# Four scheduling edits in a two-layer attention trunk: halved weight casts, two earlier bias tables, earlier rotary tables, and the cosine product of the rotary step on GpSimd

## The chip, the cores and the metric

The kernel runs on one core of a Trainium2 chip as one launch. The metric is the device time of one execution in microseconds (us), the median over runs. TensorE (PE in the profile, its weight loads PEld) does the matrix products, VectorE is DVE, ScalarE is ACT, GpSimd is POOL, and SyncE (SP) issues most of the transfers; ACT issues the weight loads.

## What is computed

An encoder trunk of two layers over 1024 tokens of width 1024, all in float32. Layer A is chunked attention with 16 heads of 64 and a learned bias by relative distance; layer B is differential attention (two softmax maps for each of 8 heads, one subtracted from the other) with rotary positions on the first quarter of each head dimension. Cut to what matters here:

```python
def partial_rope(t, positions):
    ang = positions.astype(jnp.float32)[..., None] * inv_freq
    cos, sin = jnp.cos(ang), jnp.sin(ang)
    t1, t2 = t[..., :half], t[..., half:ROT_DIM]
    return jnp.concatenate([t1 * cos - t2 * sin, t2 * cos + t1 * sin, t[..., ROT_DIM:]], axis=-1)

# layer A
q, k, v, g = jnp.split(rmsnorm(h, a_norm_pre) @ a_w_in, 4, axis=-1)
bias = jnp.take(rel_bias, rel, axis=1)
s = jnp.einsum('bhqd,bhkd->bhqk', qc, kb) * scale + bias
h = h + rmsnorm((attention(s, v) * jax.nn.silu(g)) @ a_w_out, a_norm_post)
# layer B
ks_ = partial_rope(ks_, positions); q = partial_rope(q, positions)
a = p[:, :, 0] - lam * p[:, :, 1]
h = h + rmsnorm((rmsnorm(a @ v) * jax.nn.silu(g)) @ b_w_out, b_norm_post)
```

## The kernel before, in words

Every float32 product is made of three products of rounded parts: a weight or activation is cast to a high part on ACT (`hi_of`, L189) and the remainder is subtracted on DVE (`lo_of`, L192). A projection group (`mm_group`, L269, L271, L273) is 24 matmuls of 128x512 into one of two PSUM accumulators `acc`. Activations are kept transposed in R1 and R2.

The order of the work is written out by hand in **ticks** (class `Ticks`). One tick issues the work that is due before it (`at`), then 4 matmuls of the stream of projections (`FILL`), then the work due after it by rank (`after`, `later`). So a group lasts 6 ticks. `K.later(k, f, rank)` puts f k ticks on; each engine runs its instructions strictly in the order that results. The stream is projections A, output product A, projections B, output product B; the attention of a head pair is spread over the projections of the next.

What the change touches:
- `w_split` (L199 to L203): cast and remainder of one 128x1024 slice of layer A's weights, on tick 0 and 1. The first two slices are split before the projections start.
- `Prepared.prepare` (L230 to L249): the 32 slices of layer B's weights are scaled on POOL, cut into high and low part and stored to DRAM (`wcut`) during layer A.
- `bias_build` (L441 to L454): a head's bias table. A transfer brings the skewed table to the tile `b`, `part2` completes it on DVE (L448 to L450) 7 ticks later and SP stores it to `bias_t`. The scores of the head (`scores`, L606) read it back as `bt` (L635).
- `rope` (L884 to L903), called by `doneB` for the key (kind 0) and the query (kind 1) of a head pair, in two halves of 512 tokens. ACT copies `acc` to `xs`, four transfers on SP move the rotated rows to a tile `sw` (called `w` in the code), DVE writes `acc` times the cosine to `xc`, POOL multiplies `sw` by the sine at tick 3, DVE adds the two at tick 6 (5 for the first pair, u = 0), and one tick later the sum is split into parts (`split_k`, `split_q`). For the query, `split_q` also issues two transfers on SP that copy its parts to the other half of the partitions (L520, shown as R<-R).
- `layer_b_tiles` (L869 to L880): memsets and loads of the rotary tables and the mask, 6 ticks before layer B.
- `attB` (L917): when the attention blocks of layer B start; for u = 0 block i starts max(0, 1 - i) ticks late.

A scores product goes to the one PSUM tile `sp` (L597), so the next must wait until `scores` has read it. Transposes (L165) go to three PSUM tiles `tp`.

Of the kernel before, what the change touches and what calls it, by code (L numbers as in the profile page):

```python
# [11 lines left out]
F32 = mybir.dt.float32  # L12
# [94 lines left out]
def trunk(ctx, tc, x, positions, a_norm_pre, a_w_in, a_rel_rev, a_w_out, a_norm_post,  # L107
# [90 lines left out]

    def w_split(w):  # L199
        hi, lo = w_tile("whi"), w_tile("wlo")  # L200
        K.later(0, lambda: hi_of(w, hi), 2)
        K.later(1, lambda: lo_of(w, hi, lo), 2)
        return hi, lo  # L203

    class Weights:
# [18 lines left out]
    class Prepared:  # L224
# [5 lines left out]
        def prepare(self, k):  # L230
            view, n, gain = self.specs[k]
            w = mp.tile([P, D], F32, tag="h", name="w", bufs=4)
            w3 = w.rearrange("p (c n) -> p c n", n=P)
            adma(out=w3, in_=view[n])

            def cut():
                hi = mp.tile([P, D], F32, tag="h", name="wh", bufs=4)
                K.later(0, lambda: hi_of(w, hi.bitcast(F32R)))
                K.later(1, lambda: lo_of(w, hi.bitcast(F32R), w.bitcast(F32R)), 2)
                K.later(3, lambda: [dma(out=wcut[k][:, 0, :], in_=hi), dma(out=wcut[k][:, 1, :], in_=w)])  # L240

            def scaled(half):
                c = slice(half * 4, half * 4 + 4)
                G.tensor_tensor(out=w3[:, c, :], in0=w3[:, c, :],  # L244
                                in1=gain[:, c].unsqueeze(2).broadcast_to([P, 4, P]), op=ALU.mult)

            for half in range(2):
                K.later(6 + half, lambda half=half: scaled(half), 2)
            K.later(8, cut)  # L249
# [191 lines left out]
    def bias_build(h, k):  # L441
        def part1():
            b = mp.tile([P, D], F32, tag="h", name="b", bufs=4)
            dma(out=b[:, 384:640], in_=skew[h][127:127 + P * 382].rearrange("(p x) -> p x", x=382)[:, 0:256])
            K.later(7, lambda: part2(b))

        def part2(b):
            V.tensor_copy(out=b[:, 0:384], in_=b[:, 384:385].broadcast_to([P, 384]))  # L448
            V.memset(b[64:128, 0:64], NEG)
            V.memset(b[0:64, 576:640], NEG)  # L450
            dma(out=bias_t[h][NT], in_=b[:, 0:640])

        K.later(k, lambda: bias_skew(h))
        K.later(k + 4, part1)  # L454
# [426 lines left out]

    swc = [0]

    def rope(acc, half, first, then):  # L884

        cs = slice(half * 512, (half + 1) * 512)
        xs = lp.tile([P, 512], F32, tag="px", name="xs", bufs=3)
        xc = lp.tile([P, 512], F32, tag="px", name="xc", bufs=3)
        w = rot[swc[0] % 2]
        swc[0] += 1  # L890

# [4 lines left out]
                dma(out=w[m + 8:m + 16, :], in_=xs[m:m + 8, :])  # L896

        K.later(0, a)
        K.later(0, lambda: V.tensor_tensor(out=xc, in0=acc, in1=rot["cos"][:, cs], op=ALU.mult), 2)  # L899
        k = 5 if first else 6  # L900
        K.later(3, lambda: G.tensor_tensor(out=w, in0=w, in1=rot["sin"][:, cs], op=ALU.mult))  # L901
        K.later(k, lambda: V.tensor_tensor(out=xc, in0=xc, in1=w, op=ALU.add))
        then(xc, k + 1)  # L903

    def doneB(u, kind, half, acc):
        par = u % 2
        if kind == 0:
            rope(acc, half, u == 0, lambda xs, k: split_k(xs, ksB(par)[:, :, half * 512:half * 512 + 512], k))
        elif kind == 2:
            v = vvB(par, half).rearrange("p b (l n) -> p b l n", l=2)  # L910
            v_tokens(acc, lambda pt: pt.rearrange("p (b n) -> p b n", b=4), v[:, :, 0, :], v[:, :, 1, :])
        elif kind == 1:
            rope(acc, half, u == 0, lambda xs, k: split_q(xs, qqB, half, k))
        else:
            gate(acc, gB[u])

    def attB(u, base):  # L917
        par = u % 2
        for i in range(NT):
            attB_block(u, par, i, base + 6 * i + (max(0, 1 - i) if u == 0 else 0))  # L920

    def attB_block(u, par, i, t0):
        w = (i + 1) * P
# [153 lines left out]
    for k in range(32):  # L1077
        K.after(START + 30 + 21 * k // 2, lambda k=k: WB.prepare(k))
    K.after(start_b - 14, lambda: WB.load(0))
    K.after(start_b - 6, layer_b_tiles)  # L1080
    K.after(start_b - 11, lambda: WB.split(0))
    for O, w, R, t0, lead in ((OA, w_out_a, R1, out_a, 6), (OB, w_out_b, R2, out_b, 7)):
        wout(w, R, 0, t0 - 19)
# [99 lines left out]
```

## Time and profile before

| | |
|---|---|
| median of 3 runs | 1328.13 us (1327.79 to 1331.78) |
| the profiled execution | 1329.67 us |
| its span in the trace | 1327.8 us |
| PE busy | 1290.0 us, 97% |
| DVE, ACT, POOL busy | 826.2, 685.1, 450.2 us |

The span runs from the first to the last instruction that the trace shows; 1.9 us of the execution lie outside it. Layer A's projections and attention run to about 560 us of the span, its output product to 677, layer B's projections and attention to about 1190, and its output product to the end. In a view of waits, an instruction is followed by what it waited for; in a timeline a row gives start, duration, engine, line, operation and tiles, and in brackets the idle time of the engine just before it with what ended it. The granted clock of PE has two levels, 1.2 and 2.4 GHz, shown as 0.5 and 1.0.

### The profile page before, as it was taken

The page shows a single profiled execution, that of the slowest core. Times are in us where ns is not written, and L with a number is a line of the kernel's source. Part 1 is how long each engine was busy: PE and PEld are TensorE (multiplying, and loading weights), DVE is VectorE, ACT ScalarE, POOL GpSimd, SP SyncE. Part 2 cuts the span into 40 slices and gives each one's busy share as a digit, 9 for nine tenths or more (in the row PEclk, how much of TensorE's full clock was granted, in tenths as well). Part 3 has the DMA queues.
Part 4 walks back from the last instruction along what each step waited for, and adds up shares of the span by engine and source line. Part 5 has one row for each costly group of instructions (what it writes and reads, how often), then busy time and mean ns, then how long its engine had stood idle before and what let it go on. Part 6 is the DMA issues. An engine that isn't in the chain of part 4 may idle for free.

```text
span 1327.8 us, 20645 instructions
## 1 busy us (share of the span) xinstructions
PE 1290.0 (97%) x6919; PEld 1090.8 (82%) x6919; DVE 826.2 (62%) x1719; ACT 685.1 (52%) x1488; POOL 450.2 (34%) x688
## 2 busy tenths in 40 slices
PE   6899999999999999999997999999999999999997
PEld 5788888888888888888886888888888888888786
DVE  5466665656575656665434676757575758588643
ACT  5456575656565656654333454545454545456311
POOL 1146444555545454442221222212121212122321
PEclk8999999999999999999998999999999999999999
DMA  5477767776677778655443232323232323225343
GB/s 215 117 259 226 229 216 233 242 233 231 229 251 246 236 223 268 205 176 151 148 134 115 77 107 73 107 76 108 75 109 74 109 74 109 74 78 172 99 151 107
DMA packets 103094, 211.24 MB, mean 159 GB/s; under 512 B 14432, under 2 KB 49280, under 8 KB 102976
## 3 DMA queue, kind: packets, MB, share of 16 engines
q1 hardware_dynamic: 80448, 135.85, 32.7%
q10 hardware_dynamic: 22528, 73.95, 17.2%
q8 instruction: 57, 0.93, 0.3%
q14 instruction: 61, 0.50, 0.1%
HBM read 135.19 MB, written 58.83 MB: 146 GB/s over the span
## 4 chain that ended last, share of the span: by engine, by line
PE 80%; issue 5%; POOL 5%; DVE 3%; ACT 2%; DMA 2%; SPq 1%; ACTq 0%; POOLq 0%; DVEq 0%
PE acc L269 15%; PE acc L271 14%; PE acc L273 14%; PE acc L782 12%; PE sp L597 8%; PE tp L165 8%; PE av L981 4%; PE av L699 4%; POOL st L169 1%; POOL s L651 1%; DVE R L192 1%; POOL w L244 1%; DMA skew<-rev 1%; ACT R L189 1%; DMA sw<-xs 0%
## 5 line engine op out<-in xcount | busy, mean ns | idle before, releaser
L273 PE MATMUL acc<-R,wlo 128*128 128x512 f32 x1008 | 410.4, 407 | 0.0
L269 PE MATMUL acc<-R,whi 128*128 128x512 f32 x1008 | 405.4, 402 | 0.7 <-DVE xc L899 0.7
L271 PE MATMUL acc<-R,whi 128*128 128x512 f32 x1008 | 404.7, 401 | 0.1
L612 ACT ACTIVATE s<-s,st 128x640 f32<-128x640 f32 (+7 forms) x256 | 188.2, 735 | 135.1 <-DVE st L606 131.5
L192 DVE TENSOR_TENSOR R<-tp,R 128x512 fp32r<-128x512 f32 (+3 forms) x304 | 178.8, 602 | 85.3 <-ACT R L189 83.9
L169 POOL TENSOR_TENSOR st<-st,mone 128x1 f32<-128x1 f32 x192 | 128.2, 668 | 277.5 <-ACT s L612 254.9
L273 PEld LDWEIGHTS acc<-R,wlo 128*128 128x128 f32 x1008 | 191.1, 190 | 33.0
L271 PEld LDWEIGHTS acc<-R,whi 128*128 128x128 f32 x1008 | 191.4, 190 | 30.8 <-DVE R L192 0.4
L269 PEld LDWEIGHTS acc<-R,whi 128*128 128x128 f32 x1008 | 191.7, 190 | 29.0 <-DVE xc L899 1.1
L189 ACT CAST R<-tp 128x512 fp32r<-128x512 f32 (+3 forms) x304 | 155.3, 515 | 107.6 <-PE tp L165 104.3
L597 PE MATMUL sp<-R 128*128 128x256 f32 (+3 forms) x768 | 174.3, 335 | 10.5 <-DVE st L606 6.3
L606 DVE CUSTOM_DVE_ANT_0 s<-sp,mask 128x256 f32<-128x256 f32 (+7 forms) x128 | 96.6, 755 | 111.3 <-PE sp L597 111.2
L597 PEld LDWEIGHTS sp<-R 128*128 128x128 f32 x768 | 136.4, 189 | 32.4 <-DVE st L606 8.1
L782 PE MATMUL acc<-R,ohi 128*128 128x512 f32 x512 | 161.0, 394 | 0.0
L606 DVE CUSTOM_DVE_ANT_0 s<-sp,bt 128x640 f32<-128x640 f32 (+4 forms) x128 | 83.7, 654 | 75.0 <-PE sp L597 50.0
L165 PEld LDWEIGHTS tp<-ident,s 128*128 128x128 f32 x768 | 96.0, 140 | 39.1 <-DVE s L950 10.6
L165 PE MATMUL tp<-ident,s 128*128 128x128 f32 x768 | 124.1, 274 | 0.9 <-DVE s L950 0.8
L901 POOL TENSOR_TENSOR sw<-sw,sin 128x512 f32<-128x512 f32 x32 | 43.0, 1344 | 225.0 <-DMA sw<-xs 203.9
L782 PEld LDWEIGHTS acc<-R,ohi 128*128 128x128 f32 x512 | 94.7, 188 | 18.5
L178 POOL TENSOR_SCALAR st<-st 128x1 f32<-128x1 f32 x80 | 20.7, 259 | 242.7 <-ACT tt L185 190.0
L782 PE MATMUL acc<-R,olo 128*128 128x512 f32 x256 | 101.5, 397 | 0.0
L651 POOL TENSOR_SCALAR s<-s,st 128x640 f32<-128x640 f32 (+4 forms) x128 | 90.7, 708 | 12.6
(123 smaller groups left out, 1639.2 us busy)
## 6 DMA issues: line engine op xcount, KB each, us to landing
bt<-bias_t SPq DMA_DIRECT2D x64, 320.0 KB
R<-R SPq DMA_DIRECT2D x64, 256.0 KB
wcut<-wh SPq DMA_DIRECT2D x32, 512.0 KB
wcut<-w SPq DMA_DIRECT2D x32, 512.0 KB
whi<-wcut ACTq DMA_DIRECT2D x32, 512.0 KB
wlo<-wcut ACTq DMA_DIRECT2D x32, 512.0 KB
wst<-in_a_w_in_dram ACTq DMA_DIRECT2D x29, 512.0 KB
w<-in_kv_w_dram ACTq DMA_DIRECT2D x16, 512.0 KB
```

Of the source, the lines that this page charges most:

```text
L165: T.transpose(dst, src, ident)
L169: G.tensor_tensor(out=r, in0=a, in1=mone, op=ALU.pow)
L189: A.copy(out=hi, in_=src)
L192: V.tensor_tensor(out=lo, in0=src, in1=hi.bitcast(F32), op=ALU.subtract)
L269: T.matmul(acc, lhsT=hi[:, c, :], rhs=xT(0, c), start=(c == 0), stop=False)
L271: T.matmul(acc, lhsT=hi[:, c, :], rhs=xT(1, c), start=False, stop=False)
L273: T.matmul(acc, lhsT=lo[:, c, :], rhs=xT(0, c), start=False, stop=(c == NC - 1))
L597: T.matmul(sp[:, a:b], lhsT=q[:, l, (i % 4) * P:(i % 4 + 1) * P], rhs=ks[:, head, j0 * P + a - c0:j0 * P + b - c0], start=(l == 0), stop=( ...
L606: V.tensor_tensor_reduce(out=s[:, 0:w], in0=sp, in1=add, op0=ALU.add, op1=ALU.min, scale=-0.125, scalar=BIG, accum_out=mx)
L612: A.activation(s[:, 0:w], s[:, 0:w], AF.Exp, bias=mx, scale=-1.0, accum_out=sums)
L651: G.tensor_scalar(out=s[:, 0:w], in0=s[:, 0:w], scalar1=r, scalar2=0.5, op0=ALU.mult, op1=ALU.mult)
L782: T.matmul(y, lhsT=lhs[:, c, :], rhs=R[:, n * 8 + c, l * 512:(l + 1) * 512], start=(m == 0), stop=(m == 23))
```

## The change

The casts of a weight slice and of a prepared slice are made in two halves on successive ticks (and a prepared slice is stored one tick later). The first two bias tables are completed 4 ticks after their load and not 7. `layer_b_tiles` runs 40 ticks before layer B and not 6. In `rope` the cosine product moves from DVE (read from `acc`) to POOL (in place on `xs`, at tick 2), DVE's sum goes to `xs` too, always at tick 6, and the blocks of the first pair start one tick later.

```diff
@@ -198,8 +198,10 @@
 
     def w_split(w):
         hi, lo = w_tile("whi"), w_tile("wlo")
-        K.later(0, lambda: hi_of(w, hi), 2)
-        K.later(1, lambda: lo_of(w, hi, lo), 2)
+        for k in range(2):
+            c = slice(k * 4, k * 4 + 4)
+            K.later(k, lambda c=c: hi_of(w[:, c, :], hi[:, c, :]), 2)
+            K.later(k + 1, lambda c=c: lo_of(w[:, c, :], hi[:, c, :], lo[:, c, :]), 2)
         return hi, lo
 
     class Weights:
@@ -235,9 +237,11 @@
 
             def cut():
                 hi = mp.tile([P, D], F32, tag="h", name="wh", bufs=4)
-                K.later(0, lambda: hi_of(w, hi.bitcast(F32R)))
-                K.later(1, lambda: lo_of(w, hi.bitcast(F32R), w.bitcast(F32R)), 2)
-                K.later(3, lambda: [dma(out=wcut[k][:, 0, :], in_=hi), dma(out=wcut[k][:, 1, :], in_=w)])
+                for j in range(2):
+                    c = slice(j * 512, j * 512 + 512)
+                    K.later(j, lambda c=c: hi_of(w[:, c], hi[:, c].bitcast(F32R)), 2)
+                    K.later(j + 1, lambda c=c: lo_of(w[:, c], hi[:, c].bitcast(F32R), w[:, c].bitcast(F32R)), 2)
+                K.later(4, lambda: [dma(out=wcut[k][:, 0, :], in_=hi), dma(out=wcut[k][:, 1, :], in_=w)])
 
             def scaled(half):
                 c = slice(half * 4, half * 4 + 4)
@@ -442,7 +446,7 @@
         def part1():
             b = mp.tile([P, D], F32, tag="h", name="b", bufs=4)
             dma(out=b[:, 384:640], in_=skew[h][127:127 + P * 382].rearrange("(p x) -> p x", x=382)[:, 0:256])
-            K.later(7, lambda: part2(b))
+            K.later(4 if h < 2 else 7, lambda: part2(b))
 
         def part2(b):
             V.tensor_copy(out=b[:, 0:384], in_=b[:, 384:385].broadcast_to([P, 384]))
@@ -881,11 +885,10 @@
 
     swc = [0]
 
-    def rope(acc, half, first, then):
+    def rope(acc, half, then):
 
         cs = slice(half * 512, (half + 1) * 512)
         xs = lp.tile([P, 512], F32, tag="px", name="xs", bufs=3)
-        xc = lp.tile([P, 512], F32, tag="px", name="xc", bufs=3)
         w = rot[swc[0] % 2]
         swc[0] += 1
 
@@ -896,28 +899,27 @@
                 dma(out=w[m + 8:m + 16, :], in_=xs[m:m + 8, :])
 
         K.later(0, a)
-        K.later(0, lambda: V.tensor_tensor(out=xc, in0=acc, in1=rot["cos"][:, cs], op=ALU.mult), 2)
-        k = 5 if first else 6
+        K.later(2, lambda: G.tensor_tensor(out=xs, in0=xs, in1=rot["cos"][:, cs], op=ALU.mult))
         K.later(3, lambda: G.tensor_tensor(out=w, in0=w, in1=rot["sin"][:, cs], op=ALU.mult))
-        K.later(k, lambda: V.tensor_tensor(out=xc, in0=xc, in1=w, op=ALU.add))
-        then(xc, k + 1)
+        K.later(6, lambda: V.tensor_tensor(out=xs, in0=xs, in1=w, op=ALU.add))
+        then(xs, 6 + 1)
 
     def doneB(u, kind, half, acc):
         par = u % 2
         if kind == 0:
-            rope(acc, half, u == 0, lambda xs, k: split_k(xs, ksB(par)[:, :, half * 512:half * 512 + 512], k))
+            rope(acc, half, lambda xs, k: split_k(xs, ksB(par)[:, :, half * 512:half * 512 + 512], k))
         elif kind == 2:
             v = vvB(par, half).rearrange("p b (l n) -> p b l n", l=2)
             v_tokens(acc, lambda pt: pt.rearrange("p (b n) -> p b n", b=4), v[:, :, 0, :], v[:, :, 1, :])
         elif kind == 1:
-            rope(acc, half, u == 0, lambda xs, k: split_q(xs, qqB, half, k))
+            rope(acc, half, lambda xs, k: split_q(xs, qqB, half, k))
         else:
             gate(acc, gB[u])
 
     def attB(u, base):
         par = u % 2
         for i in range(NT):
-            attB_block(u, par, i, base + 6 * i + (max(0, 1 - i) if u == 0 else 0))
+            attB_block(u, par, i, base + 6 * i + (max(0, 2 - i) if u == 0 else 0))
 
     def attB_block(u, par, i, t0):
         w = (i + 1) * P
@@ -1077,7 +1079,7 @@
     for k in range(32):
         K.after(START + 30 + 21 * k // 2, lambda k=k: WB.prepare(k))
     K.after(start_b - 14, lambda: WB.load(0))
-    K.after(start_b - 6, layer_b_tiles)
+    K.after(start_b - 40, layer_b_tiles)
     K.after(start_b - 11, lambda: WB.split(0))
     for O, w, R, t0, lead in ((OA, w_out_a, R1, out_a, 6), (OB, w_out_b, R2, out_b, 7)):
         wout(w, R, 0, t0 - 19)
```

The order of the instructions moves with it. The transfers share eight semaphores in turn (DMAHW0 to DMAHW7); a transfer that takes one waits until its last user has landed. Line numbers of the changed kernel are its own. First SP's queue in the first 20 us of the projections, before, with the two rows of ACT's queue that load and cast a weight slice (`wst_1727`):

```order
L520 DMA R2_158<-R2_158 64x1024 [waits DVE_49,Activation_49]
L421 DMA lt_1701<-in_b_lambda_q1_dram 128x64 [waits DMAHW1_49]
L421 DMA lt_1701<-in_b_lambda_k1_dram 128x64
L423 DMA kvg_1395<-in_kv_norm_dram 128x8x1 [waits DMAHW6_49]
L424 DMA bng_1396<-in_b_norm_pre_dram 128x8x1 [waits DMAHW7_49]
L425 DMA fq_1397<-in_rope_freq_dram 128x1 [waits DMAHW0_49]
L635 DMA bt_1733<-bias_t0_75 128x128 [waits DMAHW1_49]
L215 DMA wst_1727<-in_a_w_in_dram 128x1024 [waits DVE_49]
L189 CAST whi_1771<-wst_1727 128x1024 [waits DMAHW1_49]
```

The same place now:

```order
L524 DMA R2_158<-R2_158 64x1024 [waits DMAHW7_49,DVE_49,Activation_49]
L425 DMA lt_1705<-in_b_lambda_q1_dram 128x64
L425 DMA lt_1705<-in_b_lambda_k1_dram 128x64
L427 DMA kvg_1395<-in_kv_norm_dram 128x8x1 [waits DMAHW5_49]
L428 DMA bng_1396<-in_b_norm_pre_dram 128x8x1 [waits DMAHW7_49]
L429 DMA fq_1397<-in_rope_freq_dram 128x1 [waits DMAHW0_49]
L639 DMA bt_1737<-bias_t0_75 128x128 [waits DMAHW1_49]
L217 DMA wst_1731<-in_a_w_in_dram 128x1024 [waits DMAHW6_49,DVE_49]
L189 CAST whi_1777<-wst_1731 128x512 [waits DMAHW6_49]
```

Before, the first of the small loads `lt` waited on DMAHW1, the semaphore of the weight load; now it waits on nothing, the weight load has DMAHW6, and `bng` waits for the second copy of R2 (DMAHW7).

DVE at the end of the preparation of x, before:

```order
L192 TENSOR_TENSOR R1_157<-tp_1608,R1_157 128x4x128
L192 TENSOR_TENSOR R2_158<-acc_1460,R2_158 64x512 x2
L192 TENSOR_TENSOR R1_157<-tp_1626,R1_157 128x4x128
L192 TENSOR_TENSOR R1_157<-tp_1643,R1_157 128x4x128
L192 TENSOR_TENSOR R1_157<-tp_1658,R1_157 128x4x128
L448 COPY b_1568<-b_1568 128x384
L449 MEMSET b_1568 64x64
L450 MEMSET b_1568 64x64
L448 COPY b_1570<-b_1570 128x384
L449 MEMSET b_1570 64x64
L450 MEMSET b_1570 64x64
```

And now:

```order
L192 TENSOR_TENSOR R1_157<-tp_1612,R1_157 128x4x128
L452 COPY b_1572<-b_1572 128x384
L453 MEMSET b_1572 64x64
L454 MEMSET b_1572 64x64
L452 COPY b_1574<-b_1574 128x384
L453 MEMSET b_1574 64x64
L454 MEMSET b_1574 64x64
L192 TENSOR_TENSOR R2_158<-acc_1462,R2_158 64x512 x2
L192 TENSOR_TENSOR R1_157<-tp_1630,R1_157 128x4x128
L192 TENSOR_TENSOR R1_157<-tp_1655,R1_157 128x4x128
L192 TENSOR_TENSOR R1_157<-tp_1670,R1_157 128x4x128
```

The two tables now stand ahead of the last three parts of the transposed x (tile R1).

ACT at the start of layer B, before (the casts R1<-xc are the parts of a rotated key or query):

```order
L893 COPY xs_8633<-acc_8584 128x512 [waits PE_49]
L189 CAST R2_158<-tp_8646 128x4x128 [waits PE_49]
L189 CAST R2_158<-tp_8656 128x4x128 [waits PE_49]
L189 CAST R1_157<-xc_8634 64x512 [waits DVE_49]
L189 CAST R1_157<-xc_8634 64x512
L893 COPY xs_8682<-acc_8641 128x512 [waits PE_49]
L189 CAST R1_157<-xc_8683 64x512 [waits DVE_49]
L189 CAST R1_157<-xc_8683 64x512
L893 COPY xs_8721<-acc_8692 128x512 [waits PE_49,Activation_49]
```

And now:

```order
L896 COPY xs_8761<-acc_8712 128x512 [waits PE_49]
L189 CAST R2_158<-tp_8772 128x4x128 [waits PE_49]
L189 CAST R2_158<-tp_8783 128x4x128 [waits PE_49]
L896 COPY xs_8808<-acc_8767 128x512 [waits PE_49]
L189 CAST R1_157<-xs_8761 64x512 [waits DVE_49]
L189 CAST R1_157<-xs_8761 64x512
L896 COPY xs_8846<-acc_8815 128x512 [waits PE_49]
L189 CAST R1_157<-xs_8808 64x512 [waits DVE_49]
L189 CAST R1_157<-xs_8808 64x512
```

The copy of the next accumulator now stands ahead of the casts of the rotation before it, where it stood behind them.

## Rows read from the trace of the kernel before

**Rows 1.** The profile's first part: busy time, share of the span, instructions.
```profile
PE 1290.0 (97%) x6919; PEld 1090.8 (82%) x6919; DVE 826.2 (62%) x1719; ACT 685.1 (52%) x1488; POOL 450.2 (34%) x688
```
**Rows 2.** Two stretches: busy us of PE, PEld, DVE, ACT, POOL; granted clock, DMA.
```profile
690.00:720.00 30.00, 23.00 (x91) 17.96 (x90) 12.66 (x25) 9.47 (x19) 4.91 (x5) 0.85 0.38 110
900.00:1190.00 290.00, 289.94 (x1568) 243.76 (x1567) 198.43 (x466) 150.88 (x370) 69.15 (x120) 1.00 0.30 90
```
**Rows 3.** Waits of PE over the span: us in total, times, longest.
```profile
PE sp L597 <- DVE st L606: 6.3, 3, 4.7
...
PE sp L597 <- DMA R<-R: 4.1, 1, 4.1
...
PE av L699 <- DVE ot L719: 3.5, 3, 1.9
PE tp L165 <- ACT vt L548: 2.2, 1, 2.2
PE tp L165 <- DVE R L192: 1.9, 1, 1.9
...
PE acc L269 <- DVE xc L899: 0.7, 1, 0.7
```
**Rows 4.** Timeline of PE, after its longest wait in layer A.
```profile
59.19 0.70 PE L597 MATMUL sp<-R 128*128 128x256 f32 x2 [4.69 <-DVE st L606]
59.68 0.63 PE L269 MATMUL acc<-R,whi 128*128 128x512 f32 x1
...
62.24 0.62 PE L269 MATMUL acc<-R,whi 128*128 128x512 f32 x1
```
**Rows 5.** The chain of waits, three pieces: start, us, what.
```profile
54.63 4.05 DMA bt<-bias_t
...
704.15 3.43 DMA R<-R
...
1259.70 61.37 PE acc L782 x268
```
**Rows 6.** Waits of SP's queue, 20 to 62 us.
```profile
SPq L421 <- DMA wst<-in_a_w_in_dram: 5.6, 1, 5.6
```
**Rows 7.** Timeline of DVE, 40 to 43 us.
```profile
40.92 0.35 DVE L448 COPY b<-b 128x384 f32<-128x384 f32 x1
...
42.10 1.35 DVE L192 TENSOR_TENSOR R<-acc,R 64x512 fp32r<-64x512 f32 x2
```
**Rows 8.** Groups of instructions by form: count, busy us, mean ns, idle before.
```profile
L901 POOL TENSOR_TENSOR sw<-sw,sin 128x512 f32<-128x512 f32 x32 | 43.0, 1344 | 225.0 <-DMA sw<-xs 203.9 <-DVE st L606 21.1
...
L192 DVE TENSOR_TENSOR wlo<-wst,whi 128x1024 fp32r<-128x1024 f32 x32 | 39.5, 1235 | 10.5 <-ACT whi L189 10.2
...
L899 DVE TENSOR_TENSOR xc<-acc,cos 128x512 f32<-128x512 f32 x32 | 22.1, 691 | 32.2 <-ACT xs L893 32.2
```
**Rows 9.** Timeline of ACT at the start of layer B.
```profile
683.65 0.57 ACT L893 COPY xs<-acc 128x512 f32<-128x512 f32 x1
...
690.72 1.25 ACT L189 CAST R<-xc 64x512 fp32r<-64x512 f32 x2 [3.96 <-DVE xc L902]
692.00 0.59 ACT L893 COPY xs<-acc 128x512 f32<-128x512 f32 x1
```
**Rows 10.** Timeline of POOL, the first sine product.
```profile
688.66 1.30 POOL L901 TENSOR_TENSOR sw<-sw,sin 128x512 f32<-128x512 f32 x1 [6.11 <-DMA sw<-xs]
```
**Rows 11.** Timeline of PE at the start of layer B.
```profile
707.23 0.73 PE L271 MATMUL acc<-R,whi 128*128 128x512 f32 x1
...
710.75 0.63 PE L269 MATMUL acc<-R,whi 128*128 128x512 f32 x1
...
717.92 0.63 PE L271 MATMUL acc<-R,whi 128*128 128x512 f32 x1
...
720.91 0.63 PE L273 MATMUL acc<-R,wlo 128*128 128x512 f32 x1
```
**Rows 12.** Waits of DVE, 720 to 1190 us.
```profile
DVE xc L902 <- POOL sw L901: 2.4, 5, 1.1
```

## The prediction

> **What bounds the kernel now.** Read the profile's first part first: PE is busy 97% of the span, the next engine 62% [rows 1]. Then the stretches: in layer B's middle PE works 289.94 of 290 us at full clock, with POOL busy 69 of them, while at the start of layer B it works 23 of 30 us and the granted clock falls to a mean of 0.85 [rows 2]. So time can be won or lost only where PE stands still, and in the slow clock that follows. The waits of PE name these places [rows 3]: 4.7 us in layer A for scores that DVE had not read, and at the start of layer B 0.7 us for an accumulator, 4.1 us for the copied query (R<-R) and 2.2 us for the copy `vt`. What a stop costs on top is the clock: normally a 128x512 matmul follows each 61.37/268 = 0.229 us [rows 5]; after the 4.7 us stop seven of them, from 59.68 to 62.24, follow each (62.24 - 59.68)/6 = 0.43 us, the lower level [rows 4]. That is 7 x 0.2 = 1.4 us more. At layer B's start there are nine such matmuls from 707.23 to 710.75 and eight from 717.92 to 720.91 [rows 11], 17 x 0.2 = 3.4 us.
>
> **The change, part by part.**
>
> *Casts in halves, at the start.* The first slice's remainder was one instruction of 1.235 us ahead of the transposed parts [rows 8]. Its second half now stands behind the norm of the third x tile, ahead of three parts of R1 for whose first PE waits 1.9 us [rows 3]. A 128x512 DVE instruction, such as the cosine product, costs 0.69 us [rows 8]: **+0.7 us** on the path (bounds 0, if the wait for the norm hides it, and 1.4, if both halves count).
>
> *Casts in halves, later.* 64 remainders each cost 2 x 0.69 - 1.235 = 0.145 us more on DVE, 9.3 us in all; the casts on ACT grow likewise. PE's full stretches hide it, since DVE is busy only 62%: **0**. In return shorter pieces let scores pass sooner. Without that cover it is the 9.3 us (third rival). The stores of the prepared slices go a tick later and behind some bias loads on SP; layer B reads them long after.
>
> *Bias tables 3 ticks earlier.* On DVE both tables (42.10 - 40.92 = 1.2 us [rows 7]) now stand ahead of the last three parts of R1. The second of these feeds the first group of tokens 512 to 1023, which PE starts without slack there: **+1.2 us** (bounds 0 and 1.2). The tables are not what was late. SP stood 5.6 us at the small load L421 for a weight load [rows 6], whose semaphore L421 had next in turn, and the first bias load behind it was issued at 54.63 and took 4.05 us [rows 5]; DVE could then read the scores and PE go on at 59.19 [rows 4]. In the new order L421 waits for no transfer. Take the issue 5.6 us sooner, plus the 1.9 us by which all is later: 50.9; landed at 55.0; the scores are read by 55.4. PE comes to its second scores at 59.19 - 4.69 + 1.9 = 56.4. The margin is 1 us, and `bng`'s new wait for the second R2 copy (3.43 us for such a copy [rows 5]) ends about when its turn comes. The stop goes, and its slow clock: **-4.7 - 1.4 = -6.1 us** (bounds 0 and -6.1).
>
> *Rotary tables 34 ticks earlier.* Five memsets on POOL and eight small loads on SP move into the output product of layer A. No row prices a memset; a 128x512 product of 1.34 us [rows 8] bounds it, some 7 us in all, against weight tiles that are loaded two groups (2 x 24 x 0.229 = 11 us) ahead and a POOL busy 34%: **0** (if the cover goes, up to the 7 us less the slack).
>
> *The cosine on POOL.* DVE loses 32 x 0.69 = 22 us and POOL gains 32 x 1.34 = 43 us [rows 8], both idle enough in layer B. What counts is the start. Before, ACT took the first copy at 683.65, stood 3.96 us for the sum, cast it at 690.72 and only then took the next copy at 692.00 [rows 9], and so on for four rotations; the copy `vt` stood behind the fourth, and PE behind it. Since the sum is now always at tick 6, its casts come a tick after the next copy, so ACT copies each accumulator when its group ends. Each rotation is longer: copy to product 688.66 - 683.65 = 5.0 us [rows 9, 10] (the in-place cosine waits for the transfers that read `xs`, as the sine did), then two products of 1.34: 7.7 us. The first query's group ends 24 x 0.229 = 5.5 us plus some 0.7 us of transposes after the first copy, at 689.85; its sum starts at 697.5, its first cast ends at 698.9 and the remainder at 699.5, and 3.43 us of copy [rows 5] give 703.0. PE, no longer held by the accumulator (0.7), ends two more groups at 700.8 and has eight matmuls ahead of the first scores (one tick more): 702.7. So 0.3 us remains of 4.1. `vt` is copied when its group ends. Late next are the second scores (behind the third key's parts on DVE) and the first transposes of layer B (behind the fourth rotation's sum); I price these three at 0.4 us each, under every stop after which the clock fell here. The start gives -0.7 - 4.1 - 2.2 - 3.4 + 1.2 = **-9.2 us** (bounds: +5.2, four chained rotations each 1.3 us longer, and -10.4).
>
> In the other seven pairs the sum comes 1.3 us later. DVE waits there for POOL five times, 2.4 us together [rows 12], while PE stands still for 0.06 us [rows 2]; its cosine is gone as well. I add nothing.
>
> **Sum:** 0.7 + 1.2 - 6.1 - 9.2 = -13.4 us. The profiled execution took 1329.67 us (span 1327.8, the rest around it) and would take 1316.3; it stands 1.5 us above the median, 1328.13, from which I forecast **1314.7 us**.
>
> **The rivals.**
>
> *The first stop stays.* The two earlier tables are not what PE waited for; if the bias load is still late (its 4.05 us grows, or another shared semaphore holds SP), the change does there nothing but cost 1.9 us. 1328.13 + 1.9 - 9.2 = 1320.8. For it: the margin is only 1 us. Chance 0.16.
>
> *DVE takes ACT's place at the start of layer B.* Its queue is in order too, and the second and third scores stand behind sums that now wait 1.3 us longer for POOL. Two stops of 1.3 us in place of 0.4 and one more slow clock of 9 x 0.2 return about half, 4.6 us: 1319.3. Chance 0.09.
>
> *The halved casts land on PE.* PE does wait for DVE in layer A outside the long stop (6.3 - 4.7 us for scores [rows 3]). If all 9.3 us and one slow clock (1.4) came through: 1325.4. Chance 0.09.
>
> *The slower side: POOL's second product stops PE in every later pair.* At the fourth rotation of a pair DVE already waits for the sine, 1.1 us at the worst [rows 12]; 1.3 us more puts the norm (also on POOL, behind it) and the mixing of both maps late. If some 1.7 us reach PE in each of seven pairs, with the slow clock behind: 7 x (1.7 + 1.4) = 21.7, so 1336.4. It decides once DVE's delay is longer than what it gains by the missing cosine (0.69 us) and PE's lead. Against it: PE took the present waits without a stop. The Trainium skill (GPSIMD Engine Reference, section 4.1 Engine selection) speaks for it: elementwise products belong on VectorE, being about twice as slow on GpSimd. The trace agrees on the price (1.34 against 0.69 us, [rows 8]); by that rule the move loses 21 us, and it does so only where POOL's time lies on PE's path. Chance 0.06.
>
> **How the numbers follow.** 0.60 for the forecast. A measurement of this kernel tells about 0.3% (4 us) from no change: under 1324.1 is faster, over 1332.1 slower. The forecast and the first two rivals are faster: 0.85; the third is the same: 0.09; the last slower: 0.06. The range reaches up over the first two rivals to 1323.5. Down, the three small waits (1.2), the two start costs (1.9) and half of layer A's other 5.1 us of waits for DVE (1.6 for scores, 3.5 for `av` [rows 3]) would go: 1309.
>
> **What would show it.** Right: no PE wait over 1 us between 40 and 60 us; L425 of the new kernel issued right after the second R2 copy; the four copies to `xs` 5.5 to 6.5 us apart; the waits for R<-R and `vt` under 1 us each; granted clock near 1.00 in the 30 us at layer B's start; PE full from there to the output product. Wrong: a PE stop at the first scores as long as before, copies to `xs` still 8 us apart, or PE waits for DVE in the later pairs.

## The result and the profile after

The changed kernel takes **1313.25 us** (median of 4 runs, 1312.19 to 1314.81), the kernel before in the same comparison 1329.56 us (4 runs). The ratio is 0.9877, with a 95% interval of 0.9856 to 0.9898: faster by 1.2%. The forecast was 1314.7 us in a range from 1309 to 1323.5. The profiled execution took 1312.88 us with a span of 1311.1 us, 16.7 us less than the span before; the prediction's sum was -13.4. So the time lies 1.5 us below the forecast, but the gain, by the medians of the same comparison 16.3 us, is 2.9 us larger than forecast: the kernel before came out 1.4 us above the median that the forecast started from.

The profile's first part, of the changed kernel (as [rows 1]):

```profile
PE 1280.4 (98%) x6919; PEld 1089.2 (83%) x6919; DVE 820.0 (63%) x1751; ACT 691.7 (53%) x1552; POOL 492.6 (38%) x720
```

PE's busy time has fallen by 9.6 us, though its 6919 matmuls are the same: fewer of them ran at the lower clock, and, as will be seen, waits had been counted as busy time. The waits of PE over the span (us in total, times, longest), against [rows 3]:

```profile
PE tp L165 <- DVE dev L386: 5.7, 1, 5.7
PE tp L165 <- DVE xt L484: 5.3, 3, 4.7
PE tp L165 <- DVE s L952: 3.8, 3, 3.0
PE tp L165 <- DVE R L192: 2.6, 1, 2.6
PE av L703 <- DVE ot L723: 2.3, 2, 1.9
PE sp L601 <- issue: 1.2, 1, 1.2
PE sp L601 <- DVE st L610: 1.0, 1, 1.0
PE acc L275 <- DVE R L192: 0.8, 1, 0.8
```

The first two lie nearly all in the first 15 us of the span and were there before too (5.7 and 4.9 us). Gone are the 4.7 us for scores, the 4.1 for the copied query, the 2.2 for `vt` and the 0.7 for the accumulator. New is a wait of 3.0 us for the mixing on DVE (`s`, L952). Three stretches say the same (columns as in [rows 2], where the second and third have their counterparts; the first as it was before stands ahead):

```profile
40.00:60.00 20.00, 15.21 (x67) 12.08 (x66) 6.91 (x17) 6.08 (x10) 0.26 (x1) 0.98 0.49 132
```

```profile
40.00:60.00 20.00, 18.98 (x92) 15.54 (x91) 11.57 (x25) 7.43 (x16) 2.32 (x4) 1.00 0.61 164
...
690.00:720.00 30.00, 25.75 (x115) 20.61 (x114) 12.54 (x36) 11.46 (x28) 7.39 (x9) 0.94 0.39 117
900.00:1190.00 290.00, 289.82 (x1574) 246.07 (x1573) 188.84 (x460) 153.05 (x381) 93.02 (x142) 1.00 0.29 89
```

The 30 us at the start of layer B went from 23.00 to 25.75 us of work, not to 30. The long stretch was "full" before and is now.

**The first stop.** The timeline of SP's queue in the changed kernel:

```profile
44.19 1.25 SPq L524 DMA_DIRECT2D R<-R  x2
45.48 0.58 SPq L425 DMA_DIRECT2D lt<-in_b_lambda_q_dram  x1
...
49.62 2.15 SPq L429 DMA_DIRECT2D fq<-in_rope_freq_dram  x1
52.01 1.53 SPq L639 DMA_DIRECT2D bt<-bias_t  x3
```

The first small load follows the second R2 copy at once, as forecast, and the first bias load is issued at 52.01 (forecast 50.9; before 54.63 [rows 5]). DVE reads the first scores at 54.91 (forecast 55.0 to 55.4), and PE, which comes to its second scores at 56.89, shows no wait from 44 us to one at 187.

**The start of layer B.** ACT's copies in the changed kernel, the fourth rotation on POOL and DVE, and what PE did then (the fences are the timelines of ACT, POOL, DVE and PE):

```profile
675.82 0.57 ACT L896 COPY xs<-acc 128x512 f32<-128x512 f32 x1
...
682.02 0.59 ACT L896 COPY xs<-acc 128x512 f32<-128x512 f32 x1 [3.09 <-PE acc L277]
...
687.52 0.59 ACT L896 COPY xs<-acc 128x512 f32<-128x512 f32 x1 [1.92 <-PE acc L277]
...
693.05 0.59 ACT L896 COPY xs<-acc 128x512 f32<-128x512 f32 x1 [1.67 <-issue]
```

```profile
701.62 1.28 POOL L902 TENSOR_TENSOR xs<-xs,cos 128x512 f32<-128x512 f32 x1 [5.62 <-DMA sw<-xs]
702.87 1.30 POOL L903 TENSOR_TENSOR sw<-sw,sin 128x512 f32<-128x512 f32 x1
```

```profile
704.20 0.69 DVE L904 TENSOR_TENSOR xs<-xs,sw 128x512 f32<-128x512 f32 x1 [4.20 <-POOL sw L903]
...
705.58 1.41 DVE L192 TENSOR_TENSOR R<-xs,R 64x512 fp32r<-64x512 f32 x2 [0.34 <-ACT R L189]
...
707.52 0.35 DVE L952 SCALAR_TENSOR_TENSOR s<-s,st 128x128 f32<-128x128 f32 x1
```

```profile
708.02 0.30 PE L165 MATMUL tp<-ident,s 128*128 128x128 f32 x1 [3.02 <-DVE s L952]
...
711.64 0.63 PE L273 MATMUL acc<-R,whi 128*128 128x512 f32 x1
```

The copies are now 5.5 to 6.2 us apart instead of 8.1 to 8.4, as forecast. But the fourth rotation's first product begins 8.6 us after its copy (701.62 - 693.05; the forecast took 5.0), its second stands behind that, and DVE's sum, the remainders and then the mixing stand behind both. PE waits 3.02 us for that mixing, and matmuls at the lower level (0.63 us) follow. The granted clock of 0.94 over the 30 us is one of the forecast's good signs that did not come ("near 1.00").

**Where the 16.7 us came from.** ACT's copies to `xs` cut the span into four sections: up to the first copy of layer B; from there to the first copy of its second pair; from there to that of its eighth pair (six pairs); the rest. In us, from the profiled execution of each kernel (the runs are explained below):

| kernel | to first copy | first pair | six pairs | rest | span |
|---|---|---|---|---|---|
| before | 683.65 | 63.55 | 405.72 | 174.9 | 1327.8 |
| after | 675.82 | 58.62 | 402.26 | 174.4 | 1311.1 |
| e1 bias tables | 678.39 | 62.18 | 405.69 | 174.9 | 1321.2 |
| e2 halved casts | 682.76 | 62.44 | 405.72 | 175.1 | 1326.0 |
| e3 rotary part | 684.85 | 57.24 | 402.54 | 174.4 | 1319.0 |
| e4 order alone | 685.47 | 54.85 | 405.79 | 174.9 | 1321.0 |
| e5 small loads late | 678.95 | 61.86 | 405.71 | 174.3 | 1320.8 |
| e6 first pair on DVE | 677.48 | 54.51 | 402.24 | 174.4 | 1308.6 |
| e7 cosine on DVE | 680.28 | 54.44 | 405.70 | 175.0 | 1315.4 |
| e8 as e6, first slice whole | 674.87 | 54.83 | 401.98 | 174.5 | 1306.2 |
| e9 tick 6 only | 681.83 | 53.20 | 405.78 | 175.0 | 1315.8 |
| e10 mixing late only | 685.54 | 62.31 | 405.78 | 175.0 | 1328.6 |
| e11 spare product | 675.02 | 58.54 | 404.10 | 174.4 | 1312.1 |
| e12 cosine behind mixing | 673.08 | 54.11 | 402.02 | 174.4 | 1303.6 |

So 16.7 = 7.8 (layer A) + 4.9 (start of layer B) + 3.5 (six later pairs) + 0.5. Before, e4, e9 and e10 share the code of the first section, and e3 but for the time of the rotary tables; they spread over 681.8 to 685.5 (mean 684.3): that section of one profile is good to some 2 us. The first pair, with unchanged code in before, e1, e2 and e5, spreads over 61.9 to 63.6 (mean 62.5), the last two sections over some tenths. e7's profiled execution was the slowest of its four (1317.18; the others 1311.2 to 1312.8), with a wait for scores of 3.8 us near 230 us where the other kernels with all later casts halved wait 0.9 to 1.4 us.

### The profile page after: what moved, and what is told of

Its sections match the earlier page's. It is cut to its first block, busy times and chain, and to the rows that moved or that the text cites. A ratio compares the mean times of both kernels' runs of the same rounds, so it can differ in the third digit from the quotient of the medians.

```text
span 1311.1 us, 20795 instructions
## 1 busy us (share of the span) xinstructions
PE 1280.4 (98%) x6919; PEld 1089.2 (83%) x6919; DVE 820.0 (63%) x1751; ACT 691.7 (53%) x1552; POOL 492.6 (38%) x720
## 4 chain that ended last, share of the span: by engine, by line
PE 90%; DVE 3%; ACT 2%; issue 1%; DMA 1%; POOL 1%; SPq 0%; ACTq 0%; DVEq 0%; POOLq 0%
PE acc L273 17%; PE acc L275 17%; PE acc L277 17%; PE acc L786 12%; PE sp L601 9%; PE tp L165 9%; PE av L703 5%; PE av L983 4%; DVE R L192 1%; DMA sw<-xs 1%; DMA wst<-in_a_w_in_dram 0%; ACT R L189 0%; PE acc L313 0%; DVE s L610 0%; ACT R L185 0%
## 5 line engine op out<-in xcount | busy, mean ns | idle before, releaser
L169 POOL TENSOR_TENSOR st<-st,mone 128x1 f32<-128x1 f32 x192 | 116.9, 609 | 268.1 <-ACT s L616 259.4
L902 POOL TENSOR_TENSOR xs<-xs,cos 128x512 f32<-128x512 f32 x32 | 41.4, 1294 | 187.1 <-DMA sw<-xs 142.4
L655 POOL TENSOR_SCALAR s<-s,st 128x640 f32<-128x640 f32 (+4 forms) x128 | 100.4, 785 | 12.6
```

The source lines that it names most:

```text
L169: G.tensor_tensor(out=r, in0=a, in1=mone, op=ALU.pow)
L655: G.tensor_scalar(out=s[:, 0:w], in0=s[:, 0:w], scalar1=r, scalar2=0.5, op0=ALU.mult, op1=ALU.mult)
```

## The experiments

Each time is the median of 4 to 12 runs and stands beside the median of the kernel before on the same chip; the ratio of the two comes with its 95% interval.

**e1, the bias tables alone** (kernel before):

```diff
-            K.later(7, lambda: part2(b))
+            K.later(4 if h < 2 else 7, lambda: part2(b))
```

> The kernel before with one part of the change: the first two bias tables are built 4 ticks after their load instead of 7. Theory: moving them also moves the third weight load to another place in the round of the DMA semaphores, so SP no longer stands 5.6 us at the first small load; the first bias load is issued some 4 us sooner, the 4.7 us stop of PE and its 1.4 us of slow clock go, and the tables cost 1.0 to 1.2 us ahead of the last parts of R1: 1328 to 1329 less 4.9, about 1323.5. Rival (the halved casts made the stop go): the stop stays and the tables cost 1.2 us: about 1330.

Measured: 1322.97 us against 1329.83, ratio 0.9947 (0.9933 to 0.996). The stop is gone without the casts; the tables cost PE two waits of 0.27 and 0.76 us. The theory holds, with a gain 2 us above the 4.9 us that it adds up to; e1 alone does not show where those come from.

**e2, the halved casts alone** (both hunks of the change, `w_split` and `prepare`):

```diff
-        K.later(0, lambda: hi_of(w, hi), 2)
-        K.later(1, lambda: lo_of(w, hi, lo), 2)
+        for k in range(2):
+            c = slice(k * 4, k * 4 + 4)
...
```

> The kernel before with only the casts of the weight slices in halves. Theory: the first stop of 4.7 us stays, since SP still stands at the small load; the start costs 0.7 us; the smaller waits of layer A behind DVE (1.2 at about 140 to 180 us, 1.2 at 260 to 300 us, a slow clock near 192 us) go, some 3.6 us: about 1325.5. Rival 1 (the casts are what made the first stop go): 1322 or less. Rival 2 (the halves are worth nothing or cost DVE's 9.3 us): 1329 or more.

Measured: 1328.14 us against 1329.83, ratio 0.9993 (0.9983 to 1.0003): no difference that can be told. The stop of 4.6 us stays, PE waits 2.6 us for the first part of the second x tiles, and of the later waits in layer A one of 1.2 us for `ot` and two for scores (1.2 and 0.4 us) are gone, while one of 1.1 us for scores is new: 1.7 us less. The slow clock near 192 us stays (0.72 from 192 to 198 us). The expected -3.6 us was too much, and the result lies nearer to the second rival: what the halves win later in layer A they lose at the start.

**e3, the rotary part alone** (the change's `rope`, `attB` and the time of the rotary tables):

```diff
+        K.later(2, lambda: G.tensor_tensor(out=xs, in0=xs, in1=rot["cos"][:, cs], op=ALU.mult))
+        K.later(6, lambda: V.tensor_tensor(out=xs, in0=xs, in1=w, op=ALU.add))
```

> The kernel before with only the rotary part: cosine in place on GpSimd, the sum always at tick 6, the first mixings one tick later, the rotary tables 34 ticks earlier. Theory: layer A unchanged up to the first copy of layer B; the start of layer B gives 5 us and each of the six following pairs 0.6 us (waits of 0.15 us, three or four in a pair, that PE had for the mixing on DVE): 1328 to 1329 less 8.9, about 1319.5. Rival (the later pairs gained from the casts or from something else): about 1323.5.

Measured: 1320.22 us against 1329.83, ratio 0.9917 (0.9903 to 0.9931). First pair -6.3, six pairs -3.2. The theory holds, and the three parts' gains by the medians (6.9, 1.7 and 9.6 us) add up to 18.2, where the whole gave 16.3.

**e4, the order of the rotary part without GpSimd** (kernel before, cosine still on DVE):

```diff
-        k = 5 if first else 6
+        k = 6
-            attB_block(u, par, i, base + 6 * i + (max(0, 1 - i) if u == 0 else 0))
+            attB_block(u, par, i, base + 6 * i + (max(0, 2 - i) if u == 0 else 0))
```

> The kernel before with the order of the rotary part alone: the sum at tick 6 for the first pair too, the first mixings one tick later; the cosine stays on DVE and reads the accumulator. Theory: the gain at the start of layer B is ACT's order and comes without GpSimd, 5 to 6.3 us (the fourth rotation's sum waits for one product of POOL less), while the small waits of the later pairs stay: about 1322.5. Rival (the start gains because DVE is freed of the cosine or because the copies have three buffers to themselves): 1326 or more. If the pairs are 67.0 us here too, the later gain is not DVE's load either.

Measured: 1322.17 us against 1329.83, ratio 0.994 (0.9926 to 0.9953). The first pair takes 54.85 us: 8.7 less than before, 2.4 less than with the cosine on GpSimd (e3). The six later pairs gain nothing (405.79 us).

**e5, the small loads late** (kernel before):

```diff
-    K.after(START + 14, small_loads)
+    K.after(START + 23, small_loads)
```

> The kernel before with one number changed: the eight small loads are issued 9 ticks later, behind the first two bias loads; the bias tables stay at 7 ticks, the casts and the rotary part as before. The third weight load keeps its semaphore, and now the first bias load is the one that has it next in turn. Theory (SP's queue made the first stop): SP stands the same 5.6 us, but at the bias load, which is issued near 49.6 us instead of 54.6, lands near 53.7, and the 4.7 us stop of PE with 1.4 us of slow clock goes: 1329.8 less 6.1, about 1323.7. Rival (the tables had to be built sooner, or a bias load takes that long anyhow): the stop stays, 1328 or more.

Measured: 1323.04 us against 1328.97, ratio 0.996 (0.9946 to 0.9974). SP's waits from 40 to 60 us, and its timeline:

```profile
SPq L635 <- DMA wst<-in_a_w_in_dram: 5.5, 1, 5.5
```

```profile
49.65 0.96 SPq L635 DMA_DIRECT2D bt<-bias_t  x2
50.66 0.43 SPq L421 DMA_DIRECT2D lt<-in_b_lambda_q_dram  x1
```

The bias load stands 5.5 us for the weight load, as the small load did [rows 6], but nothing stands behind that wait ahead of it, and the stop of 4.7 us is gone with the tables where they were (one of 0.9 us for later scores, at 65.5 us, is new). So the stop was made by SP's queue: a wait for a weight load, and eight small loads after it.

**e6, the first pair's cosine on DVE** (changed kernel; in `rope`, with its own `xc` where `first` is u == 0):

```diff
+        if first:
+            K.later(0, lambda: V.tensor_tensor(out=xc, in0=acc, in1=rot["cos"][:, cs], op=ALU.mult), 2)
+        else:
             K.later(2, lambda: G.tensor_tensor(out=xs, in0=xs, in1=rot["cos"][:, cs], op=ALU.mult))
```

> The changed kernel, but in the first pair the cosine stays on DVE (from the accumulator, into its own buffer); in the other seven pairs it is on GpSimd in place. Theory: the second product on GpSimd costs the start of layer B (58.62 us from the first copy to that of the second pair, against 54.85 with the cosine on DVE) and pays only in later pairs (66.97 against 67.62 us a pair): the start gets shorter by 2.4 to 3.8 us and the pairs stay at 66.97: 1313.3 less 3.1, about 1310. Rival (the start differs for another reason, such as the order of the loads of sw): 1313.

**e7, the cosine on DVE in all pairs** (changed kernel):

```diff
-        K.later(2, lambda: G.tensor_tensor(out=xs, in0=xs, in1=rot["cos"][:, cs], op=ALU.mult))
+        K.later(0, lambda: V.tensor_tensor(out=xc, in0=acc, in1=rot["cos"][:, cs], op=ALU.mult), 2)
```

> The changed kernel with the cosine on DVE in all eight pairs, everything else of the change kept. Theory: the start of layer B gets shorter by 2.4 to 3.8 us, and every later pair takes 67.62 instead of 66.97 us again, 0.65 times 6 to 7, some 4.2 us: about 1314, as the changed kernel. Rival (the move to GpSimd is what makes the rotary part gain): 1319 or more.

**e8, as e6, and the very first weight slice cast whole** (`w_split` takes the old path at its first call).

> As the run before last (the first pair's cosine on DVE), and besides the casts of the very first weight slice are whole again. Theory: the wait of PE for the first part of the second x tiles falls from 2.6 to 2.0 us, and the slow clock behind it may go with it: 0.6 to 1.3 us below that run, about 1309. Rival (that stage's time is set by the x tiles, whatever the casts): the same as that run.

Measured, beside 1328.97 us before: e6 1310.56 (0.9862, 0.9846 to 0.9877), e7 1312.22 (0.9871, 0.9856 to 0.9886), e8 1308.19 (0.9844, 0.9831 to 0.9858). With the cosine on DVE the first pair takes 54.4 to 54.8 us in all three; the later pairs are short in e6 and e8 and long in e7. So GpSimd's product costs the start 4 us and the pairs give 3.5 back: the two cancel, as expected. The first slice whole gives 2.4 us by the medians, more than expected; no run of e8 (up to 1309.86) is as slow as the fastest of e6 (1310.12). PE's wait in question is 1.6 us in e8, 2.6 in e6. **Every run of e8 is below every run of the changed kernel** (1312.19 at the least, beside a before of 1329.56), and the intervals of the two ratios overlap by no more than 0.0002: it beats both kernels.

**e9 and e10, the two numbers of e4 apart** (kernel before; e9 has the first diff line pair of e4, e10 the second).

> The kernel before with one number changed: the sum of a rotation in the first pair comes at tick 6 as in the other pairs, not at 5. The cosine stays on DVE, the first mixings stay where they were. Theory (ACT's order is the whole gain at the start of layer B): the copies to xs come 5.5 to 7 us apart instead of 8.3, and nearly all of the 8.7 us that the order gave between the first copy of layer B and that of its second pair come with this number: about 1322.5. Rival (the mixings one tick later do half of it or more): 1326 or more.

> The kernel before with one number changed: the first mixings of layer B come one tick later; the sum of the first pair stays at tick 5. Theory: the chain of copy, sum, casts and next copy on ACT stays, with copies 8.3 us apart and the waits for the copied query and for vt: about 1329, no change. Rival: 1325 or less.

Measured, beside 1329.42 us: e9 1319.77 (0.9931, 0.9914 to 0.9948), e10 1329.39 (0.9997, 0.9987 to 1.0006). ACT's timeline of e9 and of e10:

```profile
681.83 0.56 ACT L893 COPY xs<-acc 128x512 f32<-128x512 f32 x1
688.00 0.59 ACT L893 COPY xs<-acc 128x512 f32<-128x512 f32 x1 [3.08 <-PE acc L273]
693.50 0.59 ACT L893 COPY xs<-acc 128x512 f32<-128x512 f32 x1 [3.33 <-PE acc L273]
```

```profile
685.54 0.56 ACT L893 COPY xs<-acc 128x512 f32<-128x512 f32 x1
693.89 0.59 ACT L893 COPY xs<-acc 128x512 f32<-128x512 f32 x1
702.02 0.59 ACT L893 COPY xs<-acc 128x512 f32<-128x512 f32 x1
```

One number, 5 to 6, is the whole gain at the start of layer B: 10.35 us of span (63.55 to 53.20; 9.3 from the mean of 62.5), more than all that the rotary part of the change gives there. In e9 PE works 29.13 of the 30 us from 690 at full clock. The later mixing alone is worth nothing, and on top of the 6 it costs: the first pair takes 54.85 us with both numbers (e4) and 53.20 with the 6 alone. (The timed ratios, 0.994 and 0.9931, have intervals that overlap; the trace shows the cause.) DVE's timeline of e9 at the fourth rotation, with the sum, the mixing and the remainders of the rotated query:

```profile
707.33 0.69 DVE L902 TENSOR_TENSOR xc<-xc,sw 128x512 f32<-128x512 f32 x1 [2.58 <-POOL sw L901]
...
708.78 0.35 DVE L950 SCALAR_TENSOR_TENSOR s<-s,st 128x128 f32<-128x128 f32 x1
709.05 1.40 DVE L192 TENSOR_TENSOR R<-xc,R 64x512 fp32r<-64x512 f32 x2
```

Here the mixing stands ahead of the remainders, and PE does not wait for it. One tick later it stands behind their 1.4 us, as in the changed kernel's timeline above: in e4 PE waits 1.1 us for it.

**e11, a spare product on DVE** (changed kernel; `spare` is a third buffer of the ring that `xs` uses, and nobody reads it):

```diff
+        K.later(0, lambda: V.tensor_tensor(out=spare, in0=rot["cos"][:, cs], in1=rot["sin"][:, cs], op=ALU.mult), 2)
```

> The changed kernel, and DVE besides does a product of its own at each rotation, where the cosine product stood (128x512, cosine by sine table, into a buffer that nobody reads; both operands from SBUF, the accumulator is not read). Theory (the 0.65 us of a later pair are DVE's time ahead of the mixings): a pair takes about 67.6 us again instead of 66.97, and the whole is 4 to 5 us longer than the changed kernel, about 1317.5. Rival (it was DVE's reading of the accumulator, which holds PE's next group): the pairs stay at 66.97 and the time at about 1313.5.

Measured: 1313.93 us, beside 1329.42 before, ratio 0.9888 (0.9869 to 0.9907); the changed kernel has 1313.25. The six pairs take 404.10 us, between 402.26 and 405.72. Neither side holds as it was put: DVE's time is half of the 3.5 us that the six pairs had won.

**e12, the cosine on DVE, behind the mixing** (e8, with GpSimd left only the sine):

```diff
+        K.later(0 if first else 1, lambda: V.tensor_tensor(out=xc, in0=acc, in1=rot["cos"][:, cs], op=ALU.mult), 2)
```

> As the run with the first pair's cosine on DVE and the first weight slice's casts whole (1308.19 us), but in the other seven pairs too the cosine is on DVE and reads the accumulator, one tick later, so that it stands behind the scores and the mixing of that tick and not ahead of them. GpSimd has the sine alone. Theory (after the spare product gave back only 0.15 of the 0.65 us of a pair: what a pair loses is the cosine's place ahead of the scores, where DVE first waits for ACT's copy of the same accumulator): a pair takes 66.9 to 67.2 us, 1308 to 1309.5. Rival (any reading of the accumulator by DVE costs PE this): a pair takes 67.6 us, about 1312.

Measured: 1309.64 us against 1330.52, ratio 0.9845 (0.9824 to 0.9867), the same as e8. The six pairs take 402.02 us, as short as with GpSimd. What the pairs gained by was the cosine's place in DVE's queue and not its engine. Nor was it DVE's reading of the accumulator: here DVE reads it too, and later. (The expectation's 0.15 us was read from single pairs; on the sum of six, e11 gave back 1.8 of 3.5 us.)

## Why the prediction was right, and where its terms were not

The time came out 1.5 us below the forecast, inside the range. That is partly luck, since three terms were off, two one way and one the other. In the two profiles layer A was forecast at -4.2 us (0.7 + 1.2 - 6.1) and gave -7.8, the start of layer B -9.2 and gave -4.9, the later pairs 0 and gave -3.5.

**First stop, forecast -6.1 and +1.2: right** in its mechanism and, by e5, in its size. e5 gives 5.9 us without moving a table; e1 gives 6.9 with the tables' cost in it, 2 us more than the two terms together. The cost of the tables on the path, 1.0 us by PE's two waits, was foreseen as 1.2.

**Casts at the start, forecast +0.7: the wait was right, the clock behind it was left out.** PE's wait went from 1.9 [rows 3] to 2.6 us; making that slice whole again gave 2.4 us (e8 against e6). In the changed kernel's profile PE is 1.4 us later than before once that stage is over (its next wait for `xt` ends at 32.57 us instead of 31.15), twice the forecast. The granted clock from 15 to 27 us (third column from the end) goes with it in these two windows, of the changed kernel (e6 has 0.50) and of e8:

```profile
15.00:27.00 12.00, 9.40 (x45) 8.91 (x46) 9.76 (x13) 7.89 (x15) 1.74 (x6) 0.51 0.70 254
```

```profile
15.00:27.00 12.00, 10.20 (x57) 9.40 (x58) 9.71 (x13) 8.75 (x16) 2.11 (x6) 0.62 0.69 255
```

It is not the casts alone: e3, with the old casts, also had 0.51 in these 12 us, and before had 0.72; e12, with e8's casts, had 1.00. What else sets it there stays open.

**Casts later, forecast 0: some us in layer A that the sum left out.** In layer A from 60 us on PE waited 5.1 us in the kernel before and 3.3 in the changed one, 1.8 less (in e2 1.7 less). Besides, both wait 1.9 us for `ot`, until 192.4 us in the one and 187.2 us in the other, but only the kernel before has the slow clock after it: 0.28 of 6 us is 1.7 us. The two windows, of before and of the changed kernel:

```profile
191.00:197.00 6.00, 4.57 (x18) 3.98 (x19) 4.45 (x9) 4.78 (x9) 3.79 (x5) 0.72 0.44 119
```

```profile
186.00:192.00 6.00, 4.78 (x29) 4.20 (x30) 4.44 (x11) 5.76 (x12) 4.00 (x5) 1.00 0.49 126
```

These two make most of the 3.6 us by which layer A gave more than its terms. The second is no gain that the casts make sure of: e2 and e6, with the casts in halves, have 0.72 after that wait as well, so in the changed kernel's profile it may be luck. The rival that the halves land on PE (9 in 100) is out.

**Start of layer B, forecast -9.2, came -4.9: the order was right and the residual was mis-sized.** The order alone (e9) gave 9.3 to 10.35. The step that failed is the residual of three waits of 0.4 us. They measured nothing for R<-R, 1.2 us for the second scores (`sp` in the list above) and 3.0 us for the first transposes, and a slow clock from 708 to 714 us followed that the forecast had at nothing. For the transposes it took the transfers of every rotation to land as the first one's had, 5.0 us after the copy. From the end of the last transfer's issue on SP to the first product it was 1.7, 1.5, 2.7 and 5.1 us for the four rotations; the last came while weight loads and a pair of query copies were under way (DMA share 0.84 from 690 to 696 us). That these loads made it late is argued, not tried. The prediction also counted the mixing's later tick only as cover for PE ("one tick more"), where it puts the mixing behind the remainders on DVE as well. Counted from ACT's first copy, the first mixing begins after 27.0 us with the sum at tick 6 alone (e9), after 28.8 to 29.5 with the mixing a tick later too (e12, e4, e8), and after 31.7 with both products on POOL (changed kernel; e3 31.9). PE's wait for it is nothing, 0.9 to 1.4 and 3.0 us; in e3 it is 1.1, because PE comes to it later, after a wait of 1.8 us for the second scores. So of the 4.7 us by which the mixing is later than in e9, the tick makes some 1.8 to 2.6, and POOL's second product with the later transfers the rest. The whole change with the first mixings where they were was not run. The second rival, DVE in ACT's place, is what happened in part: its 4.6 us is about what went missing, though its own working (two stops of 1.3 us in place of 0.4 and 1.8 us of clock) adds up to 3.6.

**Later pairs, forecast 0, came -3.5: the term was missing.** The prediction took 289.94 busy us of 290 at full clock [rows 2] to mean that nothing could be won there. But PE did wait. Its timeline, before and after, at the same place of the fourth pair:

```profile
894.67 0.40 PE L271 MATMUL acc<-R,whi 128*128 128x512 f32 x1
895.04 0.66 PE L165 MATMUL tp<-ident,s 128*128 128x128 f32 x4
```

```profile
880.42 0.40 PE L275 MATMUL acc<-R,whi 128*128 128x512 f32 x1
880.66 0.60 PE L165 MATMUL tp<-ident,s 128*128 128x128 f32 x4
```

From the matmul to the transposes it is 0.37 us before and 0.24 after: 0.13 us late, and no idle time shown, because the matmul's modelled end covers it. In that pair three such places have 0.37 to 0.41 us, together some 0.45 us of the 0.58 that a pair gained. The view of the tile `s` shows it as a wait of the weight loads (PEld; us, times); before, after, e11 and e12, from 740 to 1200 us:

```profile
  PEld tp L165: 8.9, 21
```

```profile
  PEld tp L165: 1.2, 2
```

```profile
  PEld tp L165: 4.6, 10
```

```profile
  PEld tp L165: 0.7, 1
```

21 times is three in each of seven pairs. The Trainium skill (Perfetto Trace Analysis, section Identifying the Most-Contended Engine) says that matmul busy time is not a good measure of how close one is to the roofline, the hardware's limit, and that the busy share of the weight loads is among the better ones. The trace agrees: matmul busy time read 100% on both sides of a 0.9% gain per pair (67.62 to 67.04 us), while the weight loads were busy 84 and 85% of that stretch.

What held the mixing up stood in the prediction's own rows: the cosine cost DVE 32.2 us of idle time, waiting for ACT's copy of the same accumulator [rows 8], one time in each rotation (0.3 to 1.9 us), with the scores queued behind. Before, in the fourth pair, on ACT and on DVE:

```profile
882.44 0.59 ACT L893 COPY xs<-acc 128x512 f32<-128x512 f32 x1 [0.97 <-PE acc L273]
```

```profile
883.05 0.69 DVE L899 TENSOR_TENSOR xc<-acc,cos 128x512 f32<-128x512 f32 x1 [1.75 <-ACT xs L893]
883.66 0.95 DVE L606 CUSTOM_DVE_ANT_0 s<-sp,mask 128x768 f32<-128x768 f32 x1
```

In e12, one tick later, the row reads (line L910 in that kernel; idle time before its 32 cosine products, and times):

```profile
  ACT xs L904: 1.4, 1
```

The Trainium skill (PSUM — Partial Sum Buffer, section Terms) says that two engines may not touch one bank at once, two reads included. The trace agrees in so far as DVE's cosine never began before ACT's copy had ended: in each of the 32 rotations before it began 0.03 us after it, as at 883.05 after a copy from 882.44 of 0.59 us.

**The rivals.** That POOL's second product stops PE in every later pair (6 in 100) did not come: it costs there nothing that e8 and e12 can tell apart. The higher price of a product on POOL told in the first pair alone, where POOL's time lies on PE's path: 4 us (after against e6). The first stop staying (16 in 100) did not come, by a margin of 1.7 us: DVE was through with the first scores at 55.2, and PE came to the second at 56.89.

## What to carry to other kernels

An engine shown 100% busy can still be waiting: compare the period of a repeated stage by a marker of another engine, and read the waits of the weight loads, before a stage is called full. In a queue that runs in order, the place of an instruction can count more than its engine: here one tick for a sum (e9) was worth over 9 us, one tick for the first mixings cost 1.65 of them again (e4), and one tick for a product (e12) was worth as much as moving it to another engine, without that engine's longer path. When a part of a change helps in one stage and hurts in another, make it depend on the stage: e8 is faster than the whole change by 4 to 5 us.

## What the runs showed of the hardware that was not expected

Two reads of one accumulator by ACT and DVE ran one after the other, at 0.3 to 1.9 us of waiting on DVE in each of 32 rotations, 1.0 us in the mean. Small transfers of 8 partitions took from 1.5 to 5.1 us from the end of their issue to their use in four successive rotations of one kernel. And the granted clock at the kernel's start, over the same 12 us, differed between kernels whose code there is the same (0.72 before and 0.51 in e3; 0.62 in e8 and 1.00 in e12), so a single profile of that stage tells less than the median of several runs.
